# Both attentions of a two-layer diffusion trunk step: one more stage, and three scalings on ScalarE

## Chip, core and metric

The kernel runs on one core of one Trainium2 chip. The metric is the device time of one execution in microseconds (us); the time before is the median of 3 runs. Engines are named as in the profile: PE is TensorE's matmul stream and PEld its weight loads, DVE is VectorE, ACT ScalarE, POOL GpSimd, SP SyncE (which issues most of the loads).

## What is computed

One inference step of a trunk with two layers over 512 latent and 128 context tokens, width 2048, head dimension 128. Cut to what matters here:

```python
def attend(q, k, v, sink=None):            # per block of 128 queries
    s = einsum('bkgqd,bksd->bkgqs', qi, k) * d ** -0.5
    p = softmax(s)                         # with a sink logit in layer 0
    return einsum('bkgqs,bksv->bkgqv', p, v)

# layer 0: A, banded grouped-query attention (8 heads, 2 key heads) beside a gated short convolution
# layer 1: C, differential attention, 4 heads, two softmax maps each:
o1 = attend(cq[:, 0], ck_all[:, 0], cv_all)
o2 = attend(cq[:, 1], ck_all[:, 1], cv_all)
o_c = rms_norm(o1 - lam * o2, c_on) * (1.0 - lam_init)
# layer 1: D, grouped-query attention, 8 heads, 2 key heads, dense
```

Queries and keys are RMS-normalised by head and rotated; every branch has a SiLU gate; each layer ends in one output projection and a gated residual. Latent queries read 256 cached keys and 512 latent keys (layer 0: the cached ones and a band), context queries only the 128 context keys. So a head has five blocks of queries: four latent ones with 512 to 768 keys each and one with 128.

## The kernel before, in words

Every fp32 product is made of three matmuls on a high and a low part of each operand (`split`, L296 to L298: ACT writes the high part, DVE subtracts it for the low one). A column tile of a projection is 4 quarters of the contraction times 2 halves of 320 tokens; one half of a quarter is 12 matmuls of 128x320 (`proj_q`, L332 to L334). In the later part of each projection, pairs of columns go through a seven-product scheme (`run_pairs`, L626 to L628).

The attentions have no phase of their own: they are Python generators whose steps are put between the matmuls of the projections. `run_tiles` walks through its list of jobs, a projection column each, with a function that is begun when the column is done; after the first half of a quarter it calls `pace_attn`, after the second `slot`. `slot` first runs what earlier steps put off (`settle_late`), then one step of every generator in `prep` (keys, queries, values), then as many attention steps as `pace_attn` has credit for, then fill work for the modulation weights. The credit is `steps(i)` for job i, spread over a quarter: 1.0 in layer 0 (1.35 behind the last query), and from the table `brisk` in layer 1.

- `pair_gen` (L873) serves A and D: two query heads on one key head. Per block u it has `score(u, j)` for the two heads (matmuls L846 to L848 into the tile S, then `soft`), `groups` (transposes of the probabilities L834, split into `pth` and `ptl`) and `weigh` (value products L897 to L899). The loop has two steps for each block: scores of head 0 and transposes of the block before; then scores of head 1, the value products of the block before, and its last transposes.
- `diff_gen` (L1561) serves C: `score(u, m)` for the two maps, then, put off to the next slot, `mix` (L1581: the second map is subtracted from the first, L1585), `groups`, `weigh` (L1602 to L1604, then the scaling of the output L1606 and its squares), `norm` (L1616) and `out` (transposes L1621). Two steps for each block here too.
- `soft` (L806): row maximum of S on DVE (L808), scaled by the query's norm factor on DVE (L810; with a sink L812), Exp on ACT out of S (L815).
- S is one tile of two PSUM banks in a pool with one buffer: the next scores can be written only when Exp has read the ones before. The transposes, the value products and all small products share two PSUM buffers (T). The probabilities p have four buffers.
- `k_gen` (L670) prepares a key head: squares and gains out of the transposed keys, the norm factors on POOL (L703, L704), scaling of all five blocks by them in one DVE instruction (L706), rotation (L713 to L718), transposes back (L656), splits. It runs twice in layer 0 and ten times in layer 1. The two key heads of D come first in layer 1, through `keys_first`, two steps at a time (`in_twos`).

The framework's scheduler fixes the order on each engine when the program is built. It starts from the order of the program text and may move an instruction when it takes its operands to be late.

Of the kernel before, what the change touches and what calls it, by code (L numbers as in the profile page):

```python
# [56 lines left out]
def trunk_kernel(ctx: ExitStack, tc: tile.TileContext, I: dict, O: dict):  # L57
# [612 lines left out]
    def k_gen(ap, pp, tag, src, gain, new_out, vals=None, then=None):  # L670

        vx = []

        def v_in(j):
            vx.append(ap.tile([P, 5, P], F32, tag="stg", name="vx", bufs=2))
            nc.sync.dma_start(vx[j].rearrange("p b f -> p (b f)"), vals[1][j])

        raw = ap.tile([P, 2, P], F32, tag="ctxk", name="ctxk", bufs=1)
        nc.sync.dma_start(raw, src.rearrange("(c p) d -> p c d", p=P))
        if isinstance(pp, tuple):  # L680
            x = stage(ap, pp)
        else:
            x = ap.tile([P, NT], F32, tag="stg", name="kx", bufs=2)
            nc.sync.dma_start(x, pp)
        if vals:
            v_in(0)
        yield
        ss = small.tile([P, 5], F32, tag="ss", name="ss")
        kg = ap.tile([P, 5, P], F32, tag="rp", name="kg", bufs=3)
        junk = ap.tile([P, P * st["sets"]], BF16, tag="junk", name="junk", bufs=1)[:, 0:P]  # L690
        for sample in (True, False):
            t = to_rows(cols_of(x), sample)
            for i, b in enumerate(range(4) if sample else (4,)):
                A.activation(junk, t[:, i * P:(i + 1) * P], AF.Square, accum_out=ss[:, b:b + 1])
            if sample:
                V.tensor_mul(kg[:, 0:4, :], t.rearrange("p (b f) -> p b f", b=4),
                             gain[:, None, :].to_broadcast([P, 4, P]))
            else:
                V.tensor_mul(kg[:, 4, :], t, gain)
        if vals:  # L700
            v_in(1)
        r = small.tile([P, 5], F32, tag="r", name="r")
        G.tensor_scalar(ss, ss, 1.0 / P, EPS, ALU.mult, ALU.add)  # L703
        G.tensor_tensor(r, ss, half[:, 0:5], op=ALU.pow)  # L704
        yield
        V.tensor_mul(kg, kg, r[:, :, None].to_broadcast([P, 5, P]))  # L706
        nc.gpsimd.dma_start(new_out, kg[:, 4, :])
        m1 = ap.tile([P, 4, P], F32, tag="rp", name="m1", bufs=3)
        m2 = ap.tile([P, 4, P], F32, tag="rp", name="m2", bufs=3)
        x = kg[:, 0:4, :].rearrange("p b (a h f) -> p (b a) h f", a=2, h=2)  # L710
        y = m1.rearrange("p b (a h f) -> p (b a) h f", a=2, h=2)
        z = m2.rearrange("p b (a h f) -> p (b a) h f", a=2, h=2)
        V.tensor_mul(y, x, cosR[:, :, None, :].to_broadcast([P, 8, 2, 32]))  # L713
        yield
        V.scalar_tensor_tensor(out=z[:, :, 0, :], in0=x[:, :, 1, :], scalar=-1.0, in1=sinR,
                               op0=ALU.mult, op1=ALU.mult)
        V.tensor_mul(z[:, :, 1, :], x[:, :, 0, :], sinR)
        V.tensor_add(m1, m1, m2)  # L718
        yield
        drain(attn)  # L720
        hi, lo = (ap.tile([P, 896], F32R, tag=tag + t, name=tag + t) for t in "hl")
        st[tag] = (hi, lo)
        t = psT()
        for c in range(2):
            PE.transpose(t[:, c * P:(c + 1) * P], raw[:, c, :], ident)
        split(hi[:, 0:CTX], lo[:, 0:CTX], t[:, 0:CTX])
        t = to_rows(lambda b: kg[:, b, :], False)
        split(hi[:, CTX + NS:CTX + NT], lo[:, CTX + NS:CTX + NT], t)
        t = to_rows(lambda b: m1[:, b, :], True)
        split(hi[:, CTX:CTX + NS], lo[:, CTX:CTX + NS], t)  # L730
        if vals:
            yield
            hi, lo = st["v"] = tuple(ap.tile([P, 7, 2 * P], F32R, tag=t, name=t) for t in ("vh", "vl"))
            ctx_v(ap, vals[0], hi, lo, 2 * P)
            for j in range(2):
                cols = slice(j * P, (j + 1) * P)
                split(hi[:, 2:7, cols], lo[:, 2:7, cols], vx[j])
        if then:
            attn.append(then())
# [66 lines left out]
    def soft(ap, width, s, n, rsc, nsink=None, sink=None):  # L806
        nm = small.tile([P, 1], F32, tag="nm", name="nm")
        V.tensor_reduce(nm, s, axis=AX.X, op=ALU.max, negate=True)  # L808
        if sink is None:
            V.tensor_scalar(nm, nm, rsc, None, ALU.mult)  # L810
        else:
            V.tensor_scalar(nm, nm, rsc, nsink, ALU.mult, ALU.min)  # L812
        p = ap.tile([P, width], F32, tag="P", name="p", bufs=P_BUFS)
        l = small.tile([P, 1], F32, tag="l", name="l")
        A.activation(p[:, 0:n], s, AF.Exp, scale=rsc, bias=nm, accum_out=l)  # L815
        es = None
        if sink is not None:
            es = small.tile([P, 1], F32, tag="es", name="es", bufs=2)
            A.activation(es, sink, AF.Exp, bias=nm)
        return p, l, es  # L820
# [52 lines left out]
    def pair_gen(ap, width, k, v, qs, banded, begin, emit, done, sinks):  # L873
# [29 lines left out]
        def score(u, j):  # L903
            segs, masks, lo, hi, _ = plan(u)
            q = qs[j]
            s = scores(q, u, k, segs, masks)
            p, l, es = soft(ap, width, s[:, lo:hi], hi - lo, q[2][u], *sinks[j])
            fins.setdefault(u, []).append(later_on(
                lambda: A.activation(p[:, 0:hi - lo], p[:, 0:hi - lo], AF.Copy, scale=inverse(l, es))))
            ps.setdefault(u, []).append(p)  # L910

        for u in range(6):
            if u >= 2 and len(plan(u - 2)[4]) > 4:
                weigh(u - 2, [4])
            if u < 5:
                score(u, 0)
            if u >= 1:
                groups(u - 1, [0, 2])
            yield
            if u < 5:  # L920
                score(u, 1)
            if u >= 1:
                weigh(u - 1, [0, 2])
                groups(u - 1, [4])
            if u < 5:
                yield
        done()

# [451 lines left out]
    def twist():  # L1380
        drain(attn)
        for j in range(8):
# [3 lines left out]

    used = run_tiles(jobs, I["ev_w_in"][0], h0_maker, fill0, FILL0, ada_group, trans=TRANS, grace=GRACE,
                     cut=((0, 2), (2, 4)), summed=keep, led=even_start, lead_in=lambda: ada_on_pe(0, 0, 0, 2),
                     steps=lambda i: 0.4 if i >= n_turn else 1.35 if i > last_q else 1.0,
                     turn=(n_turn, fill0b, 0.7, tail_turn), twist=twist, fill_from=FILL0_FROM)  # L1390

    tails = [("b", "h", 3)] + [x for i in range(4, 8) for x in (("u", "c", i), ("b", "h", i))]
# [168 lines left out]
    def diff_gen(ap, h, v, kq):  # L1561
# [34 lines left out]
        def weigh(u):  # L1596
            chunks = blk_plan(u, False)[4]
            last = len(chunks) - 1
            o = psT()[:, 0:256]
            for i, c in enumerate(chunks):  # L1600
                ph, pl = (x[:, (i % 4) * P:(i % 4) * P + P] for x in pts[u][i // 4])
                PE.matmul(o, ph, v[0][:, c, :], start=(i == 0), stop=False)  # L1602
                PE.matmul(o, ph, v[1][:, c, :], start=False, stop=False)
                PE.matmul(o, pl, v[0][:, c, :], start=False, stop=(i == last))  # L1604
            on = ap.tile([P, 256], F32, tag="on", name="on", bufs=2)
            V.tensor_scalar(on, o, rls[u], None, ALU.mult)  # L1606
            ssq = small.tile([P, 1], F32, tag="ssq", name="ssq")
            junk = ap.tile([P, 256], BF16, tag="junk", name="junk")
            A.activation(junk, on, AF.Square, accum_out=ssq)
            G.tensor_scalar(ssq, ssq, 1.0 / 256, EPS, ALU.mult, ALU.add)  # L1610
            rn = rns[u] = small.tile([P, 1], F32, tag="rn", name="rn")
            G.tensor_tensor(rn, ssq, half[:, 0:1], op=ALU.pow)
            ons[u] = on
# [11 lines left out]
            else:  # L1625
                V.tensor_mul(d, x, d)

        for u in range(7):
            if u >= 2:
                norm(u - 2)  # L1630
            if u < 5:
                score(u, 0)
            if 1 <= u < 6:
                groups(u - 1)
            yield
            if u >= 2:
                out(u - 2)
            if u < 5:
                score(u, 1)
            if 1 <= u < 6:  # L1640
                weigh(u - 1)
            if u < 6:
                yield
        save_y(2 * h, 2 * h + 1)


# [96 lines left out]
    def in_twos(g):  # L1743
        while next(g, DONE) is not DONE and next(g, DONE) is not DONE:
            yield

    keys = keys_first()
    next(keys)
    prep.append(in_twos(keys))
    for h in range(4):  # L1750
        for m in range(2):
            jobs.append((OD["cq"] + (m * 4 + h) * P, q_job(f"q{m}", "c_q_norm")))
# [2 lines left out]
            jobs.append((OD["ck"] + (m * 4 + h) * P,  # L1755
                         k_job(f"k{m}", I["cache_c_k"][0, 0, m, h], "c_k_norm", O["new_c_k"][0, 0, m, h], *more)))

    brisk = {len(jobs): 1.5, len(jobs) + 1: 1.5}
    brisk.update((i, 1.5 if i < 10 else 1.1) for i in range(2, len(jobs)))
    for i in (4, 5):  # L1760
        jobs.append((OD["cg"] + i * P, very_late_gate(i, (("rp", 3), ("stg", 2), ("rp", 3)))))
    run_tiles(jobs, I["od_w_in"][0], None, fill1, FILL1, fill_from=FILL1_FROM,
# [114 lines left out]
```

## Time and profile before

| | |
|---|---|
| median of 3 runs (range) | 2270.71 us (2269.16 to 2272.91) |
| the profiled execution: time, span | 2270.89 us, 2269.1 us |
| granted TensorE clock, mean | 0.997 |
| PE / PEld busy | 2226.5 / 2147.9 us (98% / 95%) |
| DVE / ACT / POOL busy | 1720.0 / 1121.4 / 226.2 us (76% / 49% / 10%) |
| HBM read / written | 307.17 / 44.17 MB |

A row of a group gives line, engine, operation, tiles (out<-in), shape and count, then busy us and mean ns of one, then the idle time just before and what ended it. A row of the waits gives engine, tile and line, what was waited for, the sum in us, how often, and the longest. A row of the windows gives the stretch, its length, and for each engine the busy us and in brackets the number of instructions. The attention of layer 0 lies at about 200 to 550 us, that of layer 1 at about 1480 to 2070 us: D first, C from about 1740 us on. "Busy" of PE counts a matmul from start to end, and consecutive ones overlap, so short delays between them do not show in it.

### The profile page before, as it was taken

What the parts mean: (1) busy time and instruction counts of PE and PEld (TensorE: products, weight loads), DVE (VectorE), ACT (ScalarE), POOL (GpSimd) and SP (SyncE); (2) the same over time, 40 slices, a digit from 0 to 9 for tenths busy, and PEclk for the clock granted to TensorE, in tenths of its full rate; (3) what the DMA queues carried; (4) which work ended last, traced back from release to release, by engine and by line L of the source; (5) the groups of instructions that cost most, each with busy time, mean ns of one, the idle gap of its engine ahead of it and who ended that gap; (6) DMA issues with size and microseconds to landing.
All of it is one profiled execution on the core that took longest, in us unless ns stands there. A gap on an engine that the chain in (4) does not pass through costs nothing.

```text
span 2269.1 us, 41048 instructions
## 1 busy us (share of the span) xinstructions
PE 2226.5 (98%) x15660; PEld 2147.9 (95%) x15660; DVE 1720.0 (76%) x3093; ACT 1121.4 (49%) x2313; POOL 226.2 (10%) x341
## 2 busy tenths in 40 slices
PE   7999999999999999999999999999999999999999
PEld 5889999999999999999999999899999999999999
DVE  4659898988988978877877666595766887666765
ACT  4335553545344445444744445566764555553443
POOL 2220000000100100000200000100010211111010
PEclk9999999999999999999999999999999999999999
DMA  9985556565553427753763333432424343246641
GB/s 358 332 289 160 165 166 208 169 184 161 156 157 117 142 87 221 214 147 107 261 200 108 120 109 109 156 105 63 120 85 147 105 118 113 78 142 200 184 133 48
DMA packets 377189, 354.03 MB, mean 156 GB/s; under 512 B 17170, under 2 KB 324848, under 8 KB 376480
## 3 DMA queue, kind: packets, MB, share of 16 engines
q1 hardware_dynamic: 360272, 291.07, 42.7%
q0 software_dynamic: 15856, 58.11, 7.2%
q8 instruction: 123, 2.02, 0.4%
q10 hardware_dynamic: 864, 2.23, 0.3%
q14 instruction: 74, 0.61, 0.1%
HBM read 307.17 MB, written 44.17 MB: 155 GB/s over the span
## 4 chain that ended last, share of the span: by engine, by line
PE 80%; DVE 6%; DMA 6%; ACT 4%; issue 3%; POOL 1%; SPq 0%; DVEq 0%; ACTq 0%; POOLq 0%
PE pq L626 10%; PE pq L628 10%; PE pq L627 10%; PE pa L332 6%; PE pa L333 6%; PE pb L332 6%; PE pb L333 6%; PE pb L334 6%; PE pa L334 6%; PE T L834 2%; DMA adaw<-in_ada_w 1%; DVE wl L298 1%; PE S L846 1%; PE T L656 1%; PE T L178 1%
## 5 line engine op out<-in xcount | busy, mean ns | idle before, releaser
L297 ACT ACTIVATE wh<-raw 128x512 fp32r<-128x512 f32 (+1 forms) x388 | 233.3, 603 | 361.3 <-PE pb L333 246.4
L332 PE MATMUL pa<-h,wh 128*128 128x320 f32 x1152 | 367.3, 319 | 0.2 <-DVE sum L425 0.2
L333 PE MATMUL pa<-h,wh 128*128 128x320 f32 x1152 | 359.6, 312 | 0.9 <-DVE h L298 0.9
L332 PE MATMUL pb<-h,wh 128*128 128x320 f32 x1152 | 359.6, 313 | 0.9 <-ACT h L297 0.9
L334 PE MATMUL pb<-h,wl 128*128 128x320 f32 x1152 | 358.0, 311 | 0.7 <-DVE wl L298 0.7
L333 PE MATMUL pb<-h,wh 128*128 128x320 f32 x1152 | 358.4, 311 | 0.0
L334 PE MATMUL pa<-h,wl 128*128 128x320 f32 x1152 | 358.1, 311 | 0.0
L298 DVE TENSOR_TENSOR wl<-raw,wh 128x512 fp32r<-128x512 f32 (+1 forms) x388 | 253.2, 653 | 119.9 <-ACT wh L297 105.9
L626 PE MATMUL pq<-h,wh 128*128 128x320 f32 x960 | 297.7, 310 | 0.0
L627 PE MATMUL pq<-h,wh 128*128 128x320 f32 x960 | 296.6, 309 | 0.0
L628 PE MATMUL pq<-h,wl 128*128 128x320 f32 x960 | 296.4, 309 | 0.0
L332 PEld LDWEIGHTS pa<-h,wh 128*128 128x128 f32 x1152 | 216.9, 188 | 11.4 <-issue 10.3
L626 PE MATMUL pq<-T,wh 128*128 128x320 f32 x720 | 223.5, 310 | 1.0 <-ACT wh L297 1.0
L628 PE MATMUL pq<-T,wl 128*128 128x320 f32 x720 | 222.6, 309 | 0.6 <-DVE wl L298 0.6
L333 PEld LDWEIGHTS pa<-h,wh 128*128 128x128 f32 x1152 | 217.1, 188 | 6.1 <-issue 4.8
L627 PE MATMUL pq<-T,wh 128*128 128x320 f32 x720 | 222.4, 309 | 0.0
L332 PEld LDWEIGHTS pb<-h,wh 128*128 128x128 f32 x1152 | 217.8, 189 | 2.1 <-ACT h L297 1.1
L333 PEld LDWEIGHTS pb<-h,wh 128*128 128x128 f32 x1152 | 217.5, 189 | 1.2 <-issue 1.2
L334 PEld LDWEIGHTS pb<-h,wl 128*128 128x128 f32 x1152 | 217.4, 189 | 1.0 <-DVE wl L298 1.0
L334 PEld LDWEIGHTS pa<-h,wl 128*128 128x128 f32 x1152 | 216.9, 188 | 1.2 <-issue 1.2
L297 ACT ACTIVATE wh<-sx 128x512 fp32r<-128x512 f32 x180 | 113.0, 633 | 156.1 <-PE pq L627 106.4
L251 DVE SCALAR_TENSOR_TENSOR acc<-adaw,sT,acc 128x1024 f32<-128x1024 f32 x150 | 189.1, 1275 | 0.0
(389 smaller groups left out, 4767.1 us busy)
## 6 DMA issues: line engine op xcount, KB each, us to landing
adaw<-in_ada_w SPq DMA_DIRECT2D x80, 512.0 KB, 3.9
raw<-in_od_w_in SPq DMA_DIRECT2D x148, 256.0 KB, 3.1
raw<-in_ev_w_in SPq DMA_DIRECT2D x130, 256.0 KB, 3.5
ada<-in_ada_w SPq DMA_DIRECT2D x11, 2048.0 KB, 13.7
adaw<-in_ada_w SPq DMA_DIRECT2D x64, 256.0 KB, 2.8
w<-in_od_w_in SPq DMA_DIRECT2D x30, 512.0 KB, 3.9
w<-in_ev_w_in SPq DMA_DIRECT2D x27, 512.0 KB, 3.9
adah<-in_ada_w SPq DMA_DIRECT2D x20, 512.0 KB, 9.3
```

Of the source, the lines that this page charges most:

```text
L178: PE.matmul(acc[32 * g:32 * g + 32, 0:wd], sT[:, kt, :], w[:, kt % m, :], start=(i < 4), stop=(i >= KT - 4), tile_position=(0, 32 * g))
L251: V.scalar_tensor_tensor(out=acc[c], in0=w, scalar=sT[:, kt, c:c + 1], in1=acc[c], op0=ALU.mult, op1=ALU.add)
L297: A.activation(hi, x, AF.Copy)
L298: V.tensor_sub(lo, x, hi)
L332: PE.matmul(ps, wh[:, i, :], hi[:, sl], start=(j == js[0] if alone else (pos == 0 and j == 0)), stop=False)
L333: PE.matmul(ps, wh[:, i, :], lo[:, sl], start=False, stop=False)
L334: PE.matmul(ps, wl[:, i, :], hi[:, sl], start=False, stop=(j == js[1] - 1 if alone else (pos == 3 and j == 3)))
L626: PE.matmul(ps, wh[:, j, :], hi, start=(first and h == 0 and j == 0), stop=False, skip_group_check=True)
L627: PE.matmul(ps, wh[:, j, :], lo, start=False, stop=False, skip_group_check=True)
L628: PE.matmul(ps, wl[:, j, :], hi, start=False, stop=(final and h == 1 and j == 3), skip_group_check=True)
L656: PE.transpose(t[:, i * P:(i + 1) * P], src(b), ident)
L834: PE.transpose(t[:, i * P:(i + 1) * P], p, ident)
```

## The change

1. In `pair_gen` the value products and the last transposes of a block move one step later, behind the next block's transposes: the loop has 7 rounds instead of 6, 14 steps instead of 12. Scores of head 0 now close a step, behind value products and transposes.
2. In `diff_gen` the value products move one step later and the output with them: 8 rounds instead of 7, 15 steps instead of 14.
3. Three scalings go from DVE to ACT: the maxima without a sink (80 instructions of 128x1), the differential outputs out of PSUM (20 of 128x256), and the keys (12 DVE instructions of 128x640 become 60 ACT instructions of 128x128).
4. The credits rise: 1.1 instead of 1.0 in layer 0, 1.6 instead of 1.5 in layer 1 (for one job more) and 1.75 instead of 1.5 at its end. The generator of D's keys is begun one slot later (`behind`).

```diff
@@ k_gen
-        V.tensor_mul(kg, kg, r[:, :, None].to_broadcast([P, 5, P]))
+        for b in range(5):
+            A.activation(kg[:, b, :], kg[:, b, :], AF.Copy, scale=r[:, b:b + 1])
@@ soft
         if sink is None:
-            V.tensor_scalar(nm, nm, rsc, None, ALU.mult)
+            A.activation(nm, nm, AF.Copy, scale=rsc)
@@ pair_gen
-        for u in range(6):
+        for u in range(7):
+            if u >= 2:
+                weigh(u - 2, [0, 2])
+                groups(u - 2, [4])
+            if u < 5:
+                score(u, 0)
+            yield
             if u >= 2 and len(plan(u - 2)[4]) > 4:
                 weigh(u - 2, [4])
             if u < 5:
-                score(u, 0)
-            if u >= 1:
+                score(u, 1)
+            if 1 <= u < 6:
                 groups(u - 1, [0, 2])
-            yield
-            if u < 5:
-                score(u, 1)
-            if u >= 1:
-                weigh(u - 1, [0, 2])
-                groups(u - 1, [4])
-            if u < 5:
+            if u < 6:
                 yield
@@ layer 0
-                     steps=lambda i: 0.4 if i >= n_turn else 1.35 if i > last_q else 1.0,
+                     steps=lambda i: 0.4 if i >= n_turn else 1.35 if i > last_q else 1.1,
@@ diff_gen
-            V.tensor_scalar(on, o, rls[u], None, ALU.mult)
+            A.activation(on, o, AF.Copy, scale=rls[u])
...
-        for u in range(7):
+        for u in range(8):
+            if u >= 3:
+                out(u - 3)
+            if 2 <= u < 7:
+                weigh(u - 2)
+            if u < 5:
+                score(u, 0)
+            if u == 7:
+                break
+            yield
             if u >= 2:
                 norm(u - 2)
             if u < 5:
-                score(u, 0)
+                score(u, 1)
             if 1 <= u < 6:
                 groups(u - 1)
             yield
-            if u >= 2:
-                out(u - 2)
-            if u < 5:
-                score(u, 1)
-            if 1 <= u < 6:
-                weigh(u - 1)
-            if u < 6:
-                yield
@@ layer 1
+    def behind(g):
+        yield
+        yield from g
...
-    prep.append(in_twos(keys))
+    prep.append(behind(in_twos(keys)))
...
-    brisk = {len(jobs): 1.5, len(jobs) + 1: 1.5}
-    brisk.update((i, 1.5 if i < 10 else 1.1) for i in range(2, len(jobs)))
+    brisk = {len(jobs): 1.75, len(jobs) + 1: 1.75}
+    brisk.update((i, 1.6 if i < 11 else 1.1) for i in range(2, len(jobs)))
```

## The prediction

> **What bounds the kernel now.** I read the busy shares first, then the windows, then the waits of the weight loads.
>
> ```profile
> span 2269.1 us, 41048 instructions
> PE 2226.5 (98%) x15660; PEld 2147.9 (95%) x15660; DVE 1720.0 (76%) x3093; ACT 1121.4 (49%) x2313; POOL 226.2 (10%) x341
> L332 PE MATMUL pa<-h,wh 128*128 128x320 f32 x1152 | 367.3, 319 | 0.2 <-DVE sum L425 0.2
> ```
> ```profile
> 800.00:850.00 50.00, 50.00 (x343) 50.00 (x342) 37.07 (x57) 21.46 (x38) 0.54 (x1) 1.00 0.31 91
> 200.00:250.00 50.00, 50.00 (x371) 48.96 (x370) 48.23 (x87) 28.10 (x59) 1.92 (x2) 1.00 0.56 165
> 1440.00:1470.00 30.00, 26.93 (x185) 24.72 (x184) 18.90 (x38) 16.45 (x49) 5.36 (x7) 1.00 0.56 176
> 1470.00:1640.00 170.00, 168.31 (x1179) 158.60 (x1178) 126.43 (x253) 119.96 (x231) 12.22 (x10) 1.00 0.33 97
> 1740.00:2070.00 330.00, 320.85 (x2233) 307.59 (x2232) 244.96 (x500) 171.14 (x414) 48.56 (x74) 1.00 0.37 112
> ```
>
> TensorE is the bound, at full granted clock (1.00 in these rows). In the undisturbed window 343 matmuls take 50 us, 0.146 us each, while the profile gives one 0.319 us from start to end. So consecutive matmuls overlap, and a stall shorter than about 0.17 us is invisible in PE's busy time. The change leaves the number and shapes of the matmuls alone. What it can win or lose is stalls only: 3.1 us of idle PE in the window of D's first keys, 1.7 in D, 9.2 in C and the end of C, and what the overlap hides. Layer 0's attention (second row) has no idle PE at all, so I cost the new stage there at nothing.
>
> The waits of the weight loads show more, because a load is shorter than a matmul. By them, over 1470 to 2070 us, then 1440 to 1470 us, then 150 to 560 us:
>
> ```profile
> PEld T L834 <- DVE p L1585: 6.7, 8, 1.3
> PEld S L846 <- ACT p L815: 6.6, 14, 1.8
> PEld T L898 <- DVE ptl L298: 1.7, 4, 0.8
> PEld T L834 <- DVE kg L696: 1.4, 2, 1.0
> PEld T L834 <- ACT p L909: 0.9, 3, 0.3
> PEld T L1602 <- DVE ptl L298: 0.6, 1, 0.6
> ...
> PEld T L656 <- ACT ls L1548: 2.1, 1, 2.1
> PEld T L656 <- DVE kg L706: 1.6, 2, 1.2
> ...
> PEld T L656 <- DVE k0l L298: 2.4, 1, 2.4
> ```
>
> There are two large ones: transposes that wait for the mixed or scaled probabilities (6.7 + 0.9 us), and scores that wait until Exp has read the one S tile (6.6 us in 14 cases).
>
> **Part 1, the added stage.** It moves the transposes behind the next scores and the value products behind the next transposes. I took the built programs' instruction order and summed PE's work between the last score matmul a block needs and its first transpose of p, at the trace's own steps: 0.146 us for 320 columns, and from start to start in the rows below 0.17 for 384, 0.12 for 256 and 0.11 for one of six transposes.
>
> ```profile
> 1560.79 0.34 PE L847 MATMUL S<-k0l,q1h 128*128 128x384 f32 x1
> 1560.96 0.34 PE L848 MATMUL S<-k0h,q1l 128*128 128x384 f32 x1
> 1561.14 0.28 PE L897 MATMUL T<-pth,vh 128*128 128x256 f32 x1
> 1561.26 0.28 PE L898 MATMUL T<-ptl,vh 128*128 128x256 f32 x1
> ...
> 2034.79 0.82 PE L834 MATMUL T<-ident,p 128*128 128x128 f32 x6
> ```
>
> In C, from the second map's scores, the mean rises from 6.0 to 9.2 us; in D it rises from 7.0 to 9.5. The longest wait is 1.3 us, the mean rise 3.2. But five of C's 20 blocks keep less than 6.7 us, the last head's first three among them, where waits could remain. I leave 0.6 us there: 7.6 becomes 0.6, **-7.0 us**. The bounds are 0 and -7.6.
>
> The other three waits on products of the same stage (1.7 + 1.4 + 0.6 = 3.7 us) come from splits read by value products and from the two shared PSUM buffers. In C the shortest cover between transposes and value products rises from 1.5 to 2.2 us, but in D the mean stays (2.9 and 3.1). I take half, **-1.8 us**; bounds 0 and -3.7.
>
> **Part 2, the S tile.** The price of the new order is that the two scores of a block come closer together, since fewer other products stand between them. Counted as above, the mean spacing falls from 3.7 to 3.4 us in D and from 4.4 to 4.05 in C. What must fit into it is the chain from the last score matmul to the end of Exp. At its best, in the trace:
>
> ```profile
> 1561.34 0.96 DVE L808 TENSOR_REDUCE nm<-S 128x1 f32<-128x768 f32 x1
> 1562.34 0.21 DVE L810 TENSOR_SCALAR nm<-nm,rq 128x1 f32<-128x1 f32 x1
> ...
> 1562.64 0.99 ACT L815 ACTIVATE p<-S,nm,rq 128x768 f32<-128x768 f32 x1 [1.11 <-DVE nm L810]
> ```
>
> From the start of L848 at 1560.96 that is 2.67 us. Elsewhere DVE puts another instruction between maximum and scaling:
>
> ```profile
> 2035.52 0.95 DVE L808 TENSOR_REDUCE nm<-S 128x1 f32<-128x768 f32 x1
> 2036.39 0.68 DVE L298 TENSOR_TENSOR ptl<-T,pth 128x512 fp32r<-128x512 f32 x1
> 2036.99 0.20 DVE L810 TENSOR_SCALAR nm<-nm,rq 128x1 f32<-128x1 f32 x1
> ```
>
> Here 0.52 us lie between the end of the maximum and the scaling; over the 64 wide scores of layer 1 that gap is 0.42 us in the mean. If every chain took c, the waits would be the sum of what the spacings fall short of c. For the order before, c = 3.25 gives 6.7 us in 14 pairs, which is the row above (6.6 us, 14). So 3.25 us is the chain to reckon with.
>
> Moving the scaling to ACT takes it out of DVE's queue. An instruction of this size costs there:
>
> ```profile
> L810 DVE TENSOR_SCALAR nm<-nm,rq 128x1 f32<-128x1 f32 x80 | 16.7, 208 | 1.1
> L819 ACT ACTIVATE es<-sink,nm 128x1 f32<-128x1 f32 x40 | 11.5, 287 | 0.0
> L815 ACT ACTIVATE p<-S,nm,rq 128x768 f32<-128x768 f32 x64 | 63.3, 989 | 41.1 <-DVE nm L810 40.8
> ```
>
> So +0.08 us against -0.42: c falls to about 2.9. With the new spacings that makes 5.3 us of waits, **-1.3 us**. If c stays at 3.25, the new order gives 11.9 (+5.3); at c = 3.55 about 19.9 (+13.3); at 2.7, 2.3 (-4.3). What queues behind the waiting scaling on ACT are weight splits and `pth` splits. ACT already stood for 40.8 us waiting for L810 in the same place, so this wait is not new, and weight splits stand three quarters, about 10 us, ahead of their use.
>
> **Part 3, keys and outputs on ACT.**
>
> ```profile
> L706 DVE TENSOR_TENSOR kg<-kg,r 128x640 f32<-128x640 f32 x12 | 9.9, 824 | 8.2 <-POOL r L704 8.2
> L909 ACT ACTIVATE p<-p,rl 128x128 f32<-128x128 f32 x16 | 6.4, 399 | 8.2 <-DVE rl L826 8.1
> L1606 DVE TENSOR_SCALAR on<-T,rl 128x256 f32<-128x256 f32 x20 | 9.6, 480 | 4.4 <-PE T L1604 4.4
> L1101 ACT COPY y<-T 128x256 f32<-128x256 f32 x15 | 5.4, 363 | 4.5 <-PE T L899 4.5
> ```
>
> Five instructions of 0.399 us replace one of 0.824: 2.0 us if nothing overlaps, 1.5 if each overlaps the next by a quarter, so 0.7 to 1.2 us more per key. In nine of the twelve keys the order leaves at least 10 us of PE work between the transposes in and the transposes back, so these nine cost nothing. Three are exposed: D's two first keys, where PE already waits for L706 (1.6 us) and the last of the five blocks is the first one transposed, and layer 0's first key, where PE waits 2.4 us at the end of the same chain. Three times 0.8: **+2.4 us**, bounds 0 and +3.6. `behind` doesn't move the first load or the first transposes of D's key in the built order, so the 2.1 us there stay. The 20 outputs swap 0.480 us for about 0.36 (L1101 is the nearest row) on an engine with room; their transposes come a stage later, so nothing.
>
> [...]
>
> DVE loses 112 instructions, 16.7 + 9.9 + 9.6 = 36 us, and ACT gains 160. DVE was 74% busy in C (244.96 of 330 us), ACT 52%. Neither is the bound, so I give no further gain. The raised credits move the work without adding any.
>
> **The sum.** -7.0 - 1.8 - 1.3 + 2.4 = -7.7 us. The profiled execution took 2270.89 us (its span 2269.1 and 1.8 around it), 0.2 above the median, 2270.7. So **2263.0 us**, 0.34% faster. A measurement of this kernel can tell about 0.2%, 4.5 us, from no change.
>
> **Rivals.** Two prices for them:
>
> ```profile
> 1563.63 0.58 ACT L297 ACTIVATE pth<-T 128x512 fp32r<-128x512 f32 x1
> ...
> 2049.20 1.01 DVE L1585 SCALAR_TENSOR_TENSOR p<-p,w 128x768 f32<-128x768 f32 x1
> ```
>
> *The S tile eats it.* The chain doesn't get shorter: what DVE put between is replaced by what ACT puts between (a `pth` split of 128x512, 0.58 us). For it: in the new order ACT has other work between scaling and Exp in some blocks. Against: the mean gap on DVE is in the trace, and in C the scores of the first map now stand behind the value products, so the mix (1.01 us on DVE) no longer runs just ahead of their maximum. At c = 3.25: -7.0 - 1.8 + 5.3 + 2.4 = -1.1, **2269.6 us**, no change.
>
> *ScalarE becomes the slow link, slower.* The scaling now waits in ACT's queue behind splits and key blocks, so the chain grows to c = 3.55: -7.0 - 1.8 + 13.3 + 2.4 = +6.9, **2277.6 us**. It decides from c of about 3.3 on, where the gains are used up. For it: D's scores are dense (spacing under 3.0 us in 13 of its 36 pairs, 8 before), and ACT is 71% busy there (119.96 of 170 us). Against: +0.08 us is all that the instruction itself costs more. [...]
>
> *More than forecast.* All waits of the two stages and of S go, and the keys' chain stays covered: -7.6 - 3.7 - 6.6 = -17.9, **2252.8 us** at most; half of S left, about 2256.
>
> *The change doesn't do what it says.* The scheduler could undo the move. The counted covers exclude that, so it has no chance of its own.
>
> **How the numbers follow.** The forecast has 0.52 (own range 2259 to 2267: keys at 0 or +3.6, half or all of the stage's other waits; of it 0.06 lies within 0.2%). The S tile rival has 0.14, slower 0.22, more than forecast 0.12. Faster by over 0.2%: 0.46 + 0.12 = 0.58. Same: 0.06 + 0.14 = 0.20. Slower: 0.22. The range, 2255 to 2276, takes in the likeliest cases and reaches into both outer ones, leaving out some 2 in 10.
>
> **What would show it.** Right: the row "T L834 <- DVE p L1585" nearly gone, fewer than 14 S waits, the rows of L656 in the window of D's first keys grown by 1 to 2 us, idle PE from 1740 us to the end of C down from 9 to 4 us or less. Wrong: the S row well over 7 us, or new waits on L1621 or L897. The forecast falls if the sum of S waits after exceeds 13 us.

## The result

The changed kernel takes 2265.5 us in the median (2263.9 to 2267.9, 10 runs), the kernel before 2270.9 (2268.3 to 2273.5, 10 runs) on the same chip. The ratio is 0.9975, 95% interval 0.9966 to 0.9985: faster by 0.25%, 5.4 us. The forecast was 2263.0 in a range of 2255 to 2276. The same kernel run again on another chip, in the last group of experiments, came to 0.9987 (0.9979 to 0.9996), so the size is known only to about a tenth of a per cent; both intervals lie below 1.

**The profile after.** Lines from 707 on stand one higher than before (L810 is L811, L1585 is L1586). The page first:

```profile
span 2265.9 us, 41110 instructions
PE 2221.5 (98%) x15660; PEld 2148.4 (95%) x15660; DVE 1693.1 (75%) x2981; ACT 1167.9 (52%) x2473; POOL 223.5 (10%) x341
```

The number of matmuls is the same, DVE has lost 27 us and ACT gained 46.5; neither bounds the kernel, as forecast. The waits of the weight loads over 1470 to 2070 us, then 1440 to 1470, then 150 to 560 (sum in us, how often, longest):

```profile
PEld S L847 <- ACT p L816: 8.8, 21, 1.9
...
PEld T L656 <- DVE k1l L298: 1.9, 3, 1.4
PEld T L1622 <- DVE kg L696: 1.3, 3, 0.6
...
PEld T L759 <- DVE ptl L298: 0.9, 1, 0.9
...
PEld T L898 <- DVE kg L696: 0.3, 1, 0.3
```
```profile
PEld T L656 <- ACT ls L1549: 2.5, 1, 2.5
PEld T L656 <- ACT kg L707: 2.0, 2, 1.4
```
```profile
PEld T L656 <- DVE k0l L298: 3.9, 2, 2.6
```

The row that led the list before, transposes waiting for the mixed probabilities (6.7 us), is gone, and so is the one for the scaled ones (0.9). At the head now stands the S tile, 8.8 us in 21 waits where it was 6.6 in 14. Keys wait more in all three windows: D's first keys (L707) 2.0 for 1.6, a key of C (`k1l`) 1.9 for 0.7, and in layer 0 a second key (3.9 in two waits for 2.4 in one). The row of C's key in the kernel before was

```profile
PEld T L656 <- DVE k1l L298: 0.7, 3, 0.2
```

The windows, in the columns of before:

```profile
1440.00:1470.00 30.00, 26.04 (x168) 23.76 (x166) 17.32 (x36) 18.53 (x58) 5.44 (x7) 0.94 0.51 163
1470.00:1640.00 170.00, 167.53 (x1185) 159.79 (x1184) 123.20 (x225) 127.50 (x259) 11.67 (x10) 1.00 0.33 99
1740.00:2070.00 330.00, 323.26 (x2260) 311.69 (x2259) 230.06 (x439) 198.45 (x507) 44.30 (x74) 1.00 0.38 116
```

C has 6.7 us of idle PE for 9.2 before; D's window 2.5 for 1.7; that of D's first keys 4.0 for 3.1, and there the granted clock reads 0.94 where it was 1.00. The time in which no weight load runs shows more: in the last row it is 330 - 311.69 = 18.3 us, for 22.4 before (330 - 307.59).

### The profile page after: what moved, and what is told of

Its sections match the earlier page's. It is cut to its first block, busy times and chain, and to the rows that moved or that the text cites. A ratio compares the mean times of both kernels' runs of the same rounds, so it can differ in the third digit from the quotient of the medians.

```text
span 2265.9 us, 41110 instructions
## 1 busy us (share of the span) xinstructions
PE 2221.5 (98%) x15660; PEld 2148.4 (95%) x15660; DVE 1693.1 (75%) x2981; ACT 1167.9 (52%) x2473; POOL 223.5 (10%) x341
## 4 chain that ended last, share of the span: by engine, by line
PE 83%; DMA 4%; issue 4%; ACT 3%; DVE 3%; POOL 1%; SPq 1%; POOLq 0%; DVEq 0%; ACTq 0%
PE pq L626 10%; PE pq L628 10%; PE pq L627 10%; PE pa L332 6%; PE pa L333 6%; PE pb L332 6%; PE pa L334 6%; PE pb L333 6%; PE pb L334 6%; PE T L835 2%; PE S L847 2%; PE S L849 1%; PE S L848 1%; PE T L178 1%; DMA ada<-in_ada_w 1%
```

## The experiments

Each run is compared with the kernel before, in five rounds; the four of a group ran on one chip, each group on another, so between groups only ratios are compared. "The scalings" are the three that the change moves to ACT. The line ahead of each diff says from which kernel it starts.

### First group: the halves of the change, and two scalings put back

**The stages alone** (from the changed kernel; the stages, the credits and `behind` stay):

```diff
-        for b in range(5):
-            A.activation(kg[:, b, :], kg[:, b, :], AF.Copy, scale=r[:, b:b + 1])
+        V.tensor_mul(kg, kg, r[:, :, None].to_broadcast([P, 5, P]))
...
-            A.activation(nm, nm, AF.Copy, scale=rsc)
+            V.tensor_scalar(nm, nm, rsc, None, ALU.mult)
...
-            A.activation(on, o, AF.Copy, scale=rls[u])
+            V.tensor_scalar(on, o, rls[u], None, ALU.mult)
```

> The added stages, the credits and the later start of D's keys stay; the three scalings go back to DVE. Theory A (the stage earns, the scalings cost): the transposes' wait for the mixed probabilities is gone as in the changed kernel (before 6.7 us), the scores' wait for Exp is near 8.7 us (the spacings of this order against a chain of 3.25 us), the keys' waits are back at 1.6 and 2.4 us; time 2262 to 2264.5 us, 0.3 to 0.4% under the kernel before. Theory B (the relief of DVE earns, the stage is a wash): within 0.1% of the kernel before, 2269 to 2272 us.

Measured: 2264.0 us, ratio 0.9964 (0.9952 to 0.9977).

**The scalings alone**: the kernel before with the lines of that diff the other way round.

> The kernel before with the three scalings on ACT and nothing else. Theory A: the transposes still wait 5 to 8 us for the mixed probabilities, the scores' wait falls from 6.6 to some 4 to 5 us, the keys' waits grow by 3 to 4 us; time 2270 to 2273 us, the same or slower than before by 0.1%. Theory B: 2264 to 2267 us, most of the gain of the whole change.

Measured: 2277.1 us, ratio 1.0020 (1.0011 to 1.0029).

**Keys back on DVE** (from the changed kernel):

```diff
-        for b in range(5):
-            A.activation(kg[:, b, :], kg[:, b, :], AF.Copy, scale=r[:, b:b + 1])
+        V.tensor_mul(kg, kg, r[:, :, None].to_broadcast([P, 5, P]))
```

> The changed kernel with the scaling of the keys alone back on DVE. Theory A (the keys' five activations are exposed in D's two first keys, in layer 0's and in one of C's): the waits of the key transposes fall to those of before (1.6 and 2.4 us in their windows) and the time by 2 to 4 us, to 2261.5 to 2263.5 us. Rival C (the key waits only stand in for others that are late at the same place, loads and PSUM buffers): under 1 us, 2264.5 to 2266 us.

Measured: 2265.1 us, ratio 0.9961 (0.9948 to 0.9975).

**Maxima back on DVE** (from the changed kernel):

```diff
-            A.activation(nm, nm, AF.Copy, scale=rsc)
+            V.tensor_scalar(nm, nm, rsc, None, ALU.mult)
```

> The changed kernel with the scaling of the maxima alone back on DVE. By the chain that fits the changed kernel's waits (3.1 us, 8.8 us in 20 pairs) against 3.25 us with the scaling on DVE and this order's spacings (8.8 us): no difference, 2265 to 2266.5 us. Rival (the maxima on ACT shorten the chain and earn): slower than the changed kernel by 2 to 4 us, 2267 to 2269.5 us. Second rival (they only crowd ACT): faster by 2 us, 2263 us.

Measured: 2267.6 us, ratio 0.9979 (0.9970 to 0.9987).

The two halves pull apart: the stages make the kernel faster by about 8 us, the scalings slower by about 5. The waits of the weight loads name the rows, over 1470 to 2070 us, then the rows of L656 over 1440 to 1470 and 150 to 560. The scalings alone:

```profile
PEld S L847 <- ACT p L816: 7.6, 16, 2.0
PEld T L656 <- DVE k1l L298: 2.0, 3, 1.5
...
PEld T L835 <- DVE p L1586: 1.7, 3, 0.9
PEld T L835 <- ACT p L910: 1.4, 5, 0.6
```
```profile
PEld T L656 <- ACT ls L1549: 3.1, 1, 3.1
PEld T L656 <- ACT kg L707: 2.6, 2, 1.4
```
```profile
PEld T L656 <- DVE k0l L298: 4.1, 2, 2.9
```

All the key rows are up on the kernel before (2.0 for 0.7, 2.6 for 1.6, 4.1 for 2.4), without any new stage: 4.0 us in all. The S row grew too (7.6 for 6.6), where the expectation had it fall. But the row of the mix fell to 1.7 from 6.7, with no stage added. So the scalings alone also shorten the wait that the stage was meant for, and a shorter row of the mix does not by itself make the kernel faster. The rows shown here do not add up to the 5 us. The granted clock may be a part of it: its mean over the runs is 0.9963, for 0.9970 before, and 0.0007 of 2272 us is by estimate 1.6 us. What else was lost is open.

With the keys back on DVE, the stages kept:

```profile
PEld T L656 <- DVE k1l L298: 0.7, 3, 0.2
```
```profile
PEld T L656 <- DVE kg L706: 1.2, 1, 1.2
```
```profile
PEld T L656 <- DVE k0l L298: 2.6, 1, 2.6
```

Against the changed kernel that is 2.0 to 1.2, 3.9 to 2.6 and, for the key of C, 1.9 to 0.7: 3.3 us less. The ratio is lower by 0.0014, 3.2 us. The two agree, but the intervals of the two ratios overlap, and the two were measured on different chips, so it is the rows that carry the verdict. For the maxima back on DVE, 0.9979 stands against 0.9975 and 0.9987 of the changed kernel: no difference that these intervals can tell.

What the scaling of a key's block costs on ACT shows in the group of the changed kernel: 391 ns, beside the 399 that the prediction took from L909. Five of them replace one instruction of 824 ns on DVE (columns: busy us, mean ns, idle time before and what ended it):

```profile
L811 ACT ACTIVATE nm<-nm,rq 128x1 f32<-128x1 f32 x80 | 23.3, 291 | 43.5 <-DVE nm L809 43.0
L707 ACT ACTIVATE kg<-kg,r 128x128 f32<-128x128 f32 x60 | 19.0, 391 | 18.4 <-POOL r L704 18.4
L1607 ACT ACTIVATE on<-T,rl 128x256 f32<-128x256 f32 x20 | 9.5, 473 | 17.4 <-PE T L1605 17.2
```

The output out of PSUM costs 473 ns on ACT against 480 on DVE, so the prediction's 0.36 us was too low. No run moves the outputs by themselves.

### Second group: one stage at a time, and the credits

**The stage of A and D alone**, credits raised, scalings on DVE: the stages-alone kernel with the loop of `diff_gen` as before.

```diff
-        for u in range(8):
-            if u >= 3:
-                out(u - 3)
-            if 2 <= u < 7:
-                weigh(u - 2)
...
+        for u in range(7):
+            if u >= 2:
+                norm(u - 2)
...
```

> All scalings on DVE, the added stage in pair_gen (A and D) alone, diff_gen (C) as before. If the gain comes from C, where nearly all waits for probabilities lay (6.7 us on the mix L1585, 0.9 on D's scaled p): most of those 6.7 us stay, S waits 6 to 9 us, time 0 to 0.1% under the kernel before (2269 to 2272 us against 2271.5). If it comes from both alike: 0.2% under.

Measured: 2265.9 us, ratio 0.9978 (0.9968 to 0.9987).

**The stage of C alone**, credits raised, scalings on DVE: the stages-alone kernel with the loop of `pair_gen` as before.

```diff
-        for u in range(7):
-            if u >= 2:
-                weigh(u - 2, [0, 2])
-                groups(u - 2, [4])
...
+        for u in range(6):
+            if u >= 2 and len(plan(u - 2)[4]) > 4:
+                weigh(u - 2, [4])
...
```

> All scalings on DVE, the added stage in diff_gen (C) alone, pair_gen as before. If the gain comes from C: the wait on the mix is gone, D's 0.9 us on scaled p stay, S waits near 7.5 us; 0.3 to 0.4% under the kernel before, the same as both stages. If from both alike: 0.2% under.

Measured: 2269.7 us, ratio 0.9995 (0.9986 to 1.0003).

**The stage of C with the maxima on ACT**, that kernel with one line more:

```diff
-            V.tensor_scalar(nm, nm, rsc, None, ALU.mult)
+            A.activation(nm, nm, AF.Copy, scale=rsc)
```

> The stage in diff_gen alone, and the maxima scaled on ACT, keys and outputs on DVE. With the chain of 3.1 us that fits the changed kernel and this order's spacings the S waits are 6.2 us, against 7.6 us with the maxima on DVE (chain 3.25): 1 us better than the kernel with the stage in C alone, 0.35 to 0.45% under the kernel before. Rival: the order's tighter short spacings and ACT's queue eat it, no difference or slower.

Measured: 2264.8 us, ratio 0.9971 (0.9961 to 0.9981).

**Both stages with the credits of before**, scalings on DVE (from the stages-alone kernel; `behind` stays):

```diff
-                     steps=lambda i: 0.4 if i >= n_turn else 1.35 if i > last_q else 1.1,
+                     steps=lambda i: 0.4 if i >= n_turn else 1.35 if i > last_q else 1.0,
...
-    brisk = {len(jobs): 1.75, len(jobs) + 1: 1.75}
-    brisk.update((i, 1.6 if i < 11 else 1.1) for i in range(2, len(jobs)))
+    brisk = {len(jobs): 1.5, len(jobs) + 1: 1.5}
+    brisk.update((i, 1.5 if i < 10 else 1.1) for i in range(2, len(jobs)))
```

> Both stages, all scalings on DVE, and the credits of the kernel before (1.0 in layer 0; 1.5 and 1.1 in layer 1). The spacings of this order fall short of a 3.25 us chain by 5.2 us instead of 8.7, so if the S tile is what the denser steps cost: S waits 5 to 6 us and 2 to 3 us faster than with the raised credits, 0.45 to 0.5% under the kernel before. Rival (the longer generators don't finish in time at the old rate, the rest runs without projections between when the next head needs its buffers): new waits on transposes or value products at the ends of the heads, the same or slower than with the raised credits by up to 5 us.

Measured: 2263.3 us, ratio 0.9966 (0.9954 to 0.9979).

As long as both stages are there, the credits make no difference that shows (0.9966 and 0.9964). But the stage of C alone gave nothing, although its row was gone. The waits over 1470 to 2070 us, the stage of A and D alone:

```profile
PEld S L846 <- ACT p L815: 6.2, 21, 0.9
PEld T L834 <- DVE p L1585: 4.0, 6, 1.0
```

and the stage of C alone:

```profile
PEld S L846 <- ACT p L815: 8.6, 22, 2.0
PEld T L834 <- ACT p L909: 2.2, 5, 0.8
```

Where the old loop of C is kept, the row of the mix is 4.0, not 6.7; where the old loop of A and D is kept, the row of the scaled probabilities has grown (2.2 for 0.9). Neither loop was touched, only its credits were. That made the credits the suspect, and the third group undoes them for each stage.

Two things speak for caution. The stage of C with the maxima on ACT differs from the stage of C alone in one line; it was 4.9 us faster on the same chip, and the two intervals do not overlap, where 1 us had been expected. The rows do not explain it: its S row is 7.9 for 8.6, its row of the scaled probabilities 2.1 for 2.2. The granted clock may be a part. Over its 11 runs the stage of C alone has a mean clock of 0.9960, the lowest of all versions, and its run at 0.998 took 2265.0 us where the four at 0.995 took 2271.0 to 2274.1; the kernel with the maxima on ACT has 0.9972 over 8 runs, the kernel before on this chip 0.9967. By estimate, 0.0012 of 2270 us is 2.7 us of the 4.9. And the profiled execution of the stage of C alone, from which its rows come, was the slowest of the 11 (2274.1 us, median 2269.7).

### Third group: the stages with the credits of before, and the changed kernel again

**The stage of C alone, credits of before**, with the diff of the credits shown above.

> The added stage in the differential attention alone, credits of before, all three scalings on VectorE; it differs from the run with the raised credits in these alone. Theory C (the raised credits hurt the old two-step order of A and D): ratio 0.996 to 0.998, clearly below the 0.9995 with raised credits. Theory D (the stage in the differential attention by itself is worth little, since what it saves at the transposes comes back at the S tile): ratio 0.9985 to 1.0.

Measured: 2265.9 us, ratio 0.9976 (0.9967 to 0.9984).

**The stage of A and D alone, credits of before**, with the same diff.

> The added stage in A and D alone, credits of before, all three scalings on VectorE. Theory C (raised credits hurt the half that has no added stage): ratio 0.9965 to 0.998, at or below the 0.9978 with raised credits. Theory D (most of the gain lies in the stage of A and D, whatever the credits): 0.997 to 0.9985. Theory E (the two halves are worth about the same, each half of the gain): 0.9975 to 0.9985, and the differential stage alone likewise.

Measured: 2270.8 us, ratio 0.9997 (0.9989 to 1.0006).

**Both stages, credits of before, maxima on ACT**, the kernel of 0.9966 with one line more:

```diff
-            V.tensor_scalar(nm, nm, rsc, None, ALU.mult)
+            A.activation(nm, nm, AF.Copy, scale=rsc)
```

> Both added stages with the credits of before, outputs and keys scaled on VectorE, the maxima on ScalarE. Theory A (the stages bring the gain, the maxima on either engine are a wash, the keys on ScalarE cost a little): 2260 to 2266 us, ratio 0.995 to 0.998 to the kernel before, the same as with the maxima on VectorE within 0.1%; the sum of the waits of scores on Exp falls a little, 9.7 to 7-9 us. Theory B (ScalarE's queue is the slow link): waits on S over 11 us and a ratio of 0.999 or more.

Measured: 2265.6 us, ratio 0.9975 (0.9964 to 0.9985).

**The changed kernel again**, with no edit.

> The changed kernel again, beside the others on one chip. Theory A (the three scalings on ScalarE take back about 0.1% of what the stages give): ratio 0.997 to 0.998, above the stages with the old credits and the maxima on ScalarE in this batch by 0.05 to 0.15%. Rival: no difference to it beyond the intervals, 0.996 to 0.997.

Measured: 2269.1 us, ratio 0.9987 (0.9979 to 0.9996).

With the credits of before it is the stage of C that carries the gain, and the stage of A and D nothing. The same view, the stage of C alone:

```profile
PEld S L846 <- ACT p L815: 7.3, 17, 1.1
...
PEld T L834 <- ACT p L909: 0.9, 3, 0.4
...
PEld T L834 <- DVE p L1585: 0.4, 1, 0.4
```

and the stage of A and D alone:

```profile
PEld S L846 <- ACT p L815: 8.4, 19, 1.5
PEld T L834 <- DVE p L1585: 8.0, 8, 2.3
```

Here rows and times agree: where the mix's row falls from 6.7 to 0.4, the time falls by 0.24%; where it stays, with 1.8 us more at the S tile, it doesn't move. So with the credits of before the stage of C is the source of the gain, and the wait that it removes is that of C's transposes for the mix. The rows of C itself, 1740 to 2070 us, bear this out. In order: the stage of C alone and the stage of A and D alone with the credits of before, the same two with raised credits, the scalings alone:

```profile
1740.00:2070.00 330.00, 324.72 (x2267) 312.25 (x2267) 246.63 (x506) 171.84 (x414) 45.20 (x74) 1.00 0.38 117
1740.00:2070.00 330.00, 319.46 (x2225) 306.33 (x2224) 244.06 (x499) 171.00 (x414) 49.57 (x74) 1.00 0.37 112
1740.00:2070.00 330.00, 325.39 (x2267) 314.00 (x2266) 250.29 (x510) 172.46 (x418) 45.42 (x75) 0.99 0.37 113
1740.00:2070.00 330.00, 323.41 (x2261) 311.28 (x2259) 246.31 (x504) 172.97 (x416) 49.21 (x74) 1.00 0.38 117
1740.00:2070.00 330.00, 322.95 (x2256) 311.19 (x2255) 231.51 (x442) 198.90 (x510) 47.58 (x72) 1.00 0.38 112
```

No weight load runs for 17.8 and 23.7 us, then 16.0 and 18.7, then 18.8; before it was 22.4. In the same 330 us 2267, 2225, 2267, 2261 and 2256 matmuls are run, 2233 before. So the stage of C shortens C with either credits. In the run where it gave nothing, the profiled execution lost the gain again outside C: over all of it, no weight load runs for 122.0 us, for 121.2 before. `behind` is in both kernels with the credits of before, so it is not what brings the gain. And C gets shorter by two other ways as well: with raised credits in its old loop, and with the scalings alone. In the changed kernel all three act at once, and their shares can't be told apart.

With raised credits the row of the mix is half as long in C's old loop (4.0 for 8.0), and the picture of the times turns round (0.9978 for A and D, 0.9995 for C). Part of that is in the rows above, but not all: the step from 0.9995 to 0.9976 is 4.3 us, the rows of `p` and S differ by 2.2 (8.6 + 2.2 against 7.3 + 0.9 + 0.4). The effect of credits on one stage alone is therefore measured, not settled; it is hardly larger than the 0.0012 by which the changed kernel itself differed between two chips.

In this last group the changed kernel and the one with the old credits and only the maxima on ACT differ by 3.5 us of median, 0.9987 against 0.9975, about what the keys cost in the first group; but these two also differ in the credits and the outputs, and the intervals overlap too. The three lowest ratios of all (0.9961, 0.9964 and 0.9966, in two groups) belong to versions with both stages and the keys on DVE, below the changed kernel; the fourth such version is the 0.9975 just named.

## Why the prediction was right, step by step

**The bound.** TensorE stalls were the whole account, and they could be read from the weight loads. This held: idle PE of C fell by 2.4 us, the time without a weight load by 4.1, the rest hidden in PE's busy time. Not all of it stayed: idle PE grew by 0.8 us in D's window and 0.9 in that of D's first keys.

**The stage's main wait, -7.0.** It was 7.6 to nothing, -7.6. The one that mattered was the mix; the third group shows this. The stages by themselves remove it: the list of the stages alone has no such row. But the scalings alone shortened it too, to 1.7.

**The stage's other waits, -1.8.** The three rows of 3.7 us (transposes and value products that wait for `ptl` and `kg`) are gone, but others of the same kind came or grew: L898 behind `kg` (0.3, none before), L759 behind `ptl` (0.9) and L1622 behind `kg` (1.3), the last two together 1.6 more than in the trace of before:

```profile
PEld T L1621 <- DVE kg L696: 0.4, 1, 0.4
...
PEld T L758 <- DVE ptl L298: 0.2, 1, 0.2
```

So -1.8 net. The half that was taken for lack of knowledge came out by luck: all three rows went and others came, not half of each.

**The S tile, -1.3: this step failed.** The row rose by 2.2. The prediction let the chain from the last score matmul to the end of Exp shrink by what DVE had put between maximum and scaling, 0.42 us. In the trace after, over the 64 wide scores of layer 1, that gap is still 0.27 us in the mean, and the scaling costs 0.29 for 0.21 us; the timeline below shows work of ACT's own in such a gap. Up to the end of Exp, taken from the start of the last score matmul, the mean went from 3.53 to 3.26 us. By the prediction's own counting, a chain of 3.1 us in the new order gives 8.8 us of waits in 20 pairs, which is the row (8.8, 21); it had taken 2.9, and 3.1 is fitted afterwards. But the counting is also cruder than the prediction held. With the maxima back on DVE and all else as in the changed kernel, the mean chain is 3.44 us, longer than 3.26, and yet the row is shorter (it is 8.8 in both traces of the changed kernel):

```profile
PEld S L847 <- ACT p L816: 7.1, 24, 0.9
```

So moving the scaling did not shorten the waits on S. For both stages with the credits of before, scalings on DVE, the counting gives 5.2 us at 3.25 us, and measured was

```profile
PEld S L846 <- ACT p L815: 9.7, 21, 1.7
```

With the maxima on ACT as well it is 9.6, no shorter. One constant chain can't carry this: of the 64 chains after the change the mean is 3.26 us, the longest 4.40. The longest wait after, 1.85 us, ends a chain in which the scaling stands on ACT behind a split (`h<-yin`) that waits for its load (timeline of the changed kernel; in brackets the idle time before and what ended it):

```profile
2037.83 0.29 DVE L809 TENSOR_REDUCE nm<-S 128x1 f32<-128x128 f32 x1
...
2040.17 0.74 ACT L297 ACTIVATE h<-yin 128x640 fp32r<-128x640 f32 x1 [2.38 <-DMA yin<-yd]
2040.82 0.28 ACT L811 ACTIVATE nm<-nm,rq 128x1 f32<-128x1 f32 x1
...
2042.21 0.19 PEld L847 LDWEIGHTS S<-k1h,q1h 128*128 128x128 f32 x1 [1.85 <-ACT p L816]
```

The maximum is ready at 2038.1, the scaling starts at 2040.8. Before the change it was Exp itself that stood behind such a split, which waited 2.04 us for its load and started at 2039.16. The prediction had named splits as what queues behind the scaling, not that a split in front of it may itself be waiting for a load.

**The keys, +2.4.** The rows give +0.4 (D), +1.5 (layer 0) and +1.2 (a key of C), +3.1 in all, and putting the keys back takes away 3.3. The size is about right by luck: the three keys held to be exposed, D's two and layer 0's first, cost 0.6 us together instead of 2.4 (0.4, and 2.6 for 2.4 in layer 0). The other 2.5 came from two of the nine keys held to be covered, layer 0's second (1.3) and one of C's (1.2).

**The sum.** -7.6 - 1.8 + 2.2 + 3.1 = -4.1, against -5.4 and, on the second chip, -3.2 measured. The forecast of -7.7 was a larger gain than either, and the S tile alone is 3.5 us of error. As a check that does not choose among rows: over the whole profiled execution no weight load runs for 117.5 us (2265.9 - 2148.4), for 121.2 before, -3.7.

**The rivals.** "The S tile eats it" had the sign of the S term right and its size too large: at 3.1 us it is +2.2, not +5.3. "ScalarE becomes the slow link" falls: with the maxima back on DVE the time was the same within the intervals. The cost of the scalings on ACT that the rows pin down is at the keys: 3.3 us of waits less with the keys back on DVE. "More than forecast" falls with the S row.

**The marks.** The mix's row gone: right. Fewer than 14 S waits: wrong, 21. The rows of L656 at D's first keys up by 1 to 2 us: short of it, 0.8 (2.5 for 2.1 and 2.0 for 1.6). Idle PE in C from 9 to 4 or less: wrong, 6.7. Of its signs of being wrong, two came: the S row is well over 7 us (8.8), and L1622, L1621 before, waits 1.3 us for `kg` where it was 0.4. The sum of 13 us at which it was to fall was not reached. So the time came out inside the range with the main wait right, while the S term had the wrong sign and two terms were right by luck.

## What to carry to other kernels

A stage added between producer and consumer pays where the trace shows a wait between these two, and here it took some back at the next resource with a single buffer (8.8 us of waits on S for 6.6); price that buffer by its longest chains, not by the mean: here the mean chain got shorter (3.26 us for 3.53) and the waits longer. Work moved to an idler engine need not be free where its result is awaited: five instructions in place of one cost 3 us here though the engine had half its time free (ACT was 52% busy). Look at what may stand in front of the moved instruction on its new engine, a load's wait above all (2.38 us here).

## What was not expected of the hardware

In the trace of the changed kernel a stall is followed by a further loss of nearly its own size. In the windows of 5 us around D's first keys, PE waits 2.2 us for a load, and in the next 5 us the granted clock is 0.66 (columns as above, the clock is the third number from the end):

```profile
PE T L656 <- DMA kx<-kd: 2.2, 1, 2.2
```
```profile
1440.00:1445.00 5.00, 3.12 (x22) 2.86 (x20) 1.96 (x6) 0.62 (x2) 0.00 (x0) 1.00 0.82 242
1445.00:1450.00 5.00, 4.65 (x23) 4.68 (x24) 1.96 (x5) 2.98 (x12) 0.68 (x2) 0.66 0.66 238
1445.40:1448.80 3.40, 3.40 (x14) 3.40 (x15) 0.79 (x2) 2.09 (x10) 0.00 (x0) 0.50 0.73 274
```

PE is busy there for 4.65 us, but with 23 matmuls, where 5 us of the undisturbed window ahead of the prediction's first waits hold some 34: by estimate a third of 5 us, 1.7 us, is lost. The last row cuts the drop out: the clock is at half, 0.50, for 3.4 us. The kernel before, with a wait of 1.9 us at the same place, kept 1.00; the stages alone, with 2.2, and the scalings alone, with 2.8, kept it too. Of the fourteen profiled executions nine show such a drop here and five don't, so much the same wait is followed by it in one and not in another.

What sets the drop off is not shown; PE was busy for 3.12 of the 5 us ahead of it. One such drop more or less in an execution is, by the estimate of 1.7 us, of the size of the differences between neighbouring experiments here. Whether they are also why the credits' effect on one stage alone stays open is not shown.
